# Rotary partner rows copied by SBUF transfers in place of permutation products

## The chip, the cores and the metric

The kernel runs on one core of a Trainium2 chip. The metric is the device time of one execution in microseconds (us). Engines are named as in the profile: PE (matrix products), PEld (its weight loads), DVE, ACT, POOL, and SP, which only issues transfers. ACT can issue transfers as well; such an issue is written ACTq.

## The reference

Two layers of a transformer block (512 tokens, width 1024) are followed by a second block with a recurrent mixer and a mixture of experts. The change touches only the attention of the two layers: of every head of 64 columns the first 16 are rotated by an angle that depends on the position.

```python
def partial_rotary(t, positions):
    inv_freq = ROPE_THETA ** (-jnp.arange(0, ROT_DIM, 2, dtype=jnp.float32) / ROT_DIM)
    ang = positions.astype(jnp.float32)[:, :, None] * inv_freq
    cos = jnp.cos(ang)[:, :, None, :]
    sin = jnp.sin(ang)[:, :, None, :]
    t1, t2, rest = tf[..., :half], tf[..., half:ROT_DIM], tf[..., ROT_DIM:]
    rot = jnp.concatenate([t1 * cos - t2 * sin, t2 * cos + t1 * sin, rest], axis=-1)
...
        proj = h @ w_in[l] + b_in[l]
        q, k, v, u = jnp.split(
            proj, [ATTN_WIDTH, ATTN_WIDTH + KV_WIDTH, ATTN_WIDTH + 2 * KV_WIDTH], axis=-1)
        q = partial_rotary(q.reshape(B, S, N_HEADS, HEAD_DIM), positions)
        k = partial_rotary(k.reshape(B, S, N_KV_HEADS, HEAD_DIM), positions)
...
        attn_out = sliding_window_attention_with_sinks(q, k, v, sinks[l])
        pool_out = causal_pool_mixer(u, pool_w[l], pool_scale[l])
        mix = jnp.concatenate([attn_out, pool_out], axis=-1) @ w_out[l]
```

The sliding window has 128 keys, there are 8 query heads and 2 key heads. The pool mixer works on the columns u of the same projection.

## The kernel before

Activations lie transposed in SBUF: features on the 128 partitions, the 512 tokens along the free axis. A block of 128 features holds two heads, and the rotated rows are 0 to 15 and 64 to 79. Every product of 32-bit numbers is made as three products of a high and a low part (`mm3`, L156 to L158); the high part is a copy by ACT (L121 for activations, L148 for weights), the low part a difference by DVE or POOL (L122, L149). Weights come in slabs of 1 MB that SP loads into three `raw` buffers; `w` is the split slab.

Each of the two layers begins with the projection (`part`, tiles `pj` and `pu`, 24 products of 128x512 for each block of 128 output columns). Five of its blocks are rotated: the keys k and the queries q0 to q3. So `rotary` (L534 to L548) runs ten times in all. One rotary before the change: ACT brings the block with its bias into `pr` (L537) and makes the high part `th` (L121); DVE makes the low part `tl` (L122); PE multiplies both with the permutation matrix `rot` into `rp` (L541, L542), which brings to each rotated row its partner row, 8 rows further up or down, with its sign; DVE multiplies `rp` with the sine table `sn1` into `ru` (L544); POOL multiplies `pr` in its own place with the cosine table `cs1` (L545); DVE adds both (L546). Then ACT and DVE split `ru` into the pair that the scores are made of (`Qh`, `Ql` for k, q0 and q1; `Gh`, `Gl` for q2 and q3).

The rotary is a generator that yields after `tl` has been issued, and `layer` writes other projection work between its two halves. The final order on each engine is that of a list scheduler that works with its own estimates of times; each engine then executes its list strictly in order. Buffers come from rings with a fixed number of places: `TA` (2 places) holds `pr`, `TB` (1) holds `ru`, `TH` and `TL` (4 each) hold the pairs `th`/`tl`. TH and TL are used by attention too: the transposed probabilities `pt` (L596) are split into `th` (L645) and `tl` (L656), and so are the pool mixer's tiles and the squares for the norms.

After q0 and q1 the first call of `attend` begins: for each of eight units the scores `sc` (L156 to L158 on `Qh`), a softmax (`s`, `nm`, `es`, `sm`; exponentials by ACT at L631), the transposes `pt`, then the product `pv` with v. Projection blocks of u and the pool mixer are put between them as filling work. In layer 0 the products of `mod` (L275, modulation of the later norms) run in the background, straight from 1 MB loads of `ada_w` (L266) in the same three `raw` buffers. `tables` (L877) makes `sn1` and `cs1` once; `load_consts` makes `rot` by five DVE instructions from the identity.

Of the kernel before, what the change touches and what calls it, by code (L numbers as in the profile page):

```python
# [10 lines left out]
F32 = mybir.dt.float32  # L11
F32R = mybir.dt.float32r
# [4 lines left out]
OP = mybir.AluOpType  # L17
# [53 lines left out]
class K:  # L71
# [95 lines left out]
    def load_consts(self):  # L167
        nc, A = self.nc, self.A
        if "c" in A:
            self.crow = self.const.tile([KB, 128], F32, name="crow")  # L170
            nc.sync.dma_start(self.crow, A["c"].rearrange("o (k p) -> (o k) p", p=128))
        t = self.const.tile([128, CONST_W], F32, name="cst")
        nc.sync.dma_start(t, A["cst"])
        self.c = {n: t[:, o:o + w] for n, (o, w) in CONST_COLS.items()}
        self.ident = self.c["ident"]
        self.ones = self.const.tile([128, 2], F32, name="ones")
        nc.vector.memset(self.ones, 1.0)
        self.rot = self.const.tile([128, 128], F32R, name="rotr")
        nc.vector.tensor_scalar(self.rot, self.ident, 0.0, None, op0=OP.mult)
        for h in (0, 64):  # L180
            nc.vector.tensor_scalar(self.rot[:, h:h + 8], self.ident[:, h + 8:h + 16], -1.0, None, op0=OP.mult)
            nc.vector.tensor_copy(self.rot[:, h + 8:h + 16], self.ident[:, h:h + 8])
        self.eps = self.const.tile([128, 1], F32, name="eps")
        nc.vector.memset(self.eps, EPS)
        self.halfpi = self.const.tile([128, 1], F32, name="halfpi")
        nc.vector.memset(self.halfpi, math.pi / 2)
# [347 lines left out]
    def rotary(self, p, bias, done):  # L534
        nc = self.nc
        t = self.blk("TA", F32, "pr")
        nc.scalar.activation(t, p, AF.Identity, bias=bias)  # L537
        th, tl = self.tsplit(t)
        yield
        p = self.ps("rp", tag="t")  # L540
        nc.tensor.matmul(p, lhsT=self.rot, rhs=th, start=True, stop=False)  # L541
        nc.tensor.matmul(p, lhsT=self.rot, rhs=tl, start=False, stop=True)  # L542
        u = self.blk("TB", F32, "ru")
        nc.vector.tensor_tensor(u, p, self.sn1, op=OP.mult)  # L544
        nc.gpsimd.tensor_tensor(t, t, self.cs1, op=OP.mult)  # L545
        nc.vector.tensor_tensor(u, u, t, op=OP.add)  # L546
        done(u)
        yield  # L548
# [326 lines left out]
                    self.norms(h, newF, gg, gs, sh, H)  # L875
        return H or newF

    B1 = dict(G=16, Q=12, U=4, TH=4, TL=4, TA=2, TB=1)
    W1 = dict(raw=3, w=4)

    def tables(self):
        nc, A = self.nc, self.A
        self.sn1, self.cs1 = self.sincos(A["positions"], self.c["inv1"], "r1")
        self.nsink = []
        for l in range(2):
            t = self.ph.tile([128, 8], F32, name=f"sink{l}")
            s = A["sinks"][l]
            nc.sync.dma_start(t, bass.AP(tensor=s.tensor, offset=s.offset, ap=[[0, 128], [1, 8]]))
            nc.vector.tensor_scalar(t, t, -1.0, None, op0=OP.mult)
            self.nsink.append(t)  # L890
# [471 lines left out]
class K3(K2):  # L1362
# [700 lines left out]
    def run(self, out, ctx):  # L2063
        self.load_consts()
        with self.phase("w1", **self.W1), ExitStack() as self.ctx, self.phase("hh", side="right", H=16):
            with self.phase("b1", side="right", **self.B1):
                H = self.block1()
# [27 lines left out]
```

## Time and profile before

| | us |
|---|---|
| median of three runs | 2533.7 (2531.62 to 2534.28) |
| the profiled execution | 2530.84 |
| its span, from first to last instruction | 2529.0 |
| PE busy in the span | 2408.8 (95%) |
| DVE / ACT / POOL busy | 1372.4 / 907.3 / 366.6 |

The profile comes from one execution, 2.9 us under the median, and 1.84 us of its time lie around the span. The mean granted clock of PE is 0.979 of full speed. The five rotaries of layer 0 lie between 64 and 101 us of the span, those of layer 1 between 642 and 672 us. In the timelines a row is: start, duration, engine, line and operation, out<-in, count; behind it in brackets the idle time of the engine before it, and what ended that.

### The profile page before, as it was taken

To read this page: it belongs to the slowest core of one execution; us is meant where nothing else is said; L and a number is where in the kernel's file an instruction comes from. 1 tells how busy PE (TensorE), PEld (TensorE's weight loads), DVE (VectorE), ACT (ScalarE), POOL (GpSimd) and SP (SyncE) were. 2 spreads that over 40 slices of the span, in tenths; PEclk is the share of its full clock that TensorE was granted. 3 is DMA by queue.
4 is the path that set the end of the run, shared out by engine and by line. 5 is a ranking of instruction groups with operands and counts; after the bars stand their busy time and mean duration, and the time that the engine had idled before them with its cause. 6 is when DMAs were issued, how large, how long until landed. Compare 5 with 4: busy or idle time off the path is not lost. (4 is left out here: it accounts for less than half of the span.)

```text
span 2529.0 us, 30517 instructions
## 1 busy us (share of the span) xinstructions
PE 2408.8 (95%) x11804; PEld 1757.0 (69%) x11804; DVE 1372.4 (54%) x2203; ACT 907.3 (36%) x1577; POOL 366.6 (14%) x358
## 2 busy tenths in 40 slices
PE   7999999999899999998999999999999999989996
PEld 3668777778788888887787787887887643433332
DVE  4867566437977233336788786356544444222224
ACT  3654232223664222224555555233332211112111
POOL 1324000005433000002332331010000000000000
PEclk9998999999998999999999999999999999999998
DMA  7531576432212233222121122222223599989995
GB/s 259 186 111 59 200 278 215 155 100 68 64 58 63 88 100 100 84 82 76 59 76 51 42 92 78 97 78 75 90 77 133 199 374 414 423 367 424 423 423 248
DMA packets 221295, 416.60 MB, mean 165 GB/s; under 512 B 11746, under 2 KB 185294, under 8 KB 193500
## 3 DMA queue, kind: packets, MB, share of 16 engines
q1 hardware_dynamic: 214752, 406.07, 44.3%
q0 software_dynamic: 2736, 5.83, 0.6%
q10 hardware_dynamic: 3660, 2.72, 0.4%
q8 instruction: 94, 1.54, 0.2%
q14 instruction: 53, 0.43, 0.0%
HBM read 414.01 MB, written 4.72 MB: 166 GB/s over the span
## 5 line engine op out<-in xcount | busy, mean ns | idle before, releaser
L149 DVE TENSOR_TENSOR w<-raw,w 128x1024 fp32r<-128x1024 f32 (+2 forms) x216 | 263.4, 1221 | 231.1 <-ACT w L148 231.1
L148 ACT ACTIVATE w<-raw 128x1024 fp32r<-128x1024 f32 (+2 forms) x228 | 229.0, 1010 | 375.0 <-PE pu L158 149.1
L156 PE MATMUL pj<-Hh,w 128*128 128x512 f32 (+1 forms) x704 | 280.8, 403 | 5.9 <-ACT Hh L392 3.5
L157 PE MATMUL pj<-Hl,w 128*128 128x512 f32 (+1 forms) x704 | 277.9, 396 | 6.8 <-DVE Hl L395 6.8
L158 PE MATMUL pj<-Hh,w 128*128 128x512 f32 (+1 forms) x704 | 274.0, 390 | 0.0
L1833 PE MATMUL gu<-ew,x 128*64 128x512 f32 (+2 forms) x1024 | 247.1, 599 | 0.0
L158 PE MATMUL po<-Gh,w 128*128 128x512 f32 (+1 forms) x608 | 212.4, 349 | 0.0
L156 PE MATMUL po<-Gh,w 128*128 128x512 f32 (+1 forms) x608 | 211.7, 349 | 0.5 <-ACT Gh L621 0.5
L157 PE MATMUL po<-Gl,w 128*128 128x512 f32 (+1 forms) x608 | 211.2, 347 | 0.0
L156 PE MATMUL pu<-Hh,w 128*128 128x512 f32 (+1 forms) x448 | 171.7, 383 | 0.1
L157 PE MATMUL pu<-Hl,w 128*128 128x512 f32 (+1 forms) x448 | 170.9, 381 | 0.0
L158 PE MATMUL pu<-Hh,w 128*128 128x512 f32 (+1 forms) x448 | 170.8, 382 | 0.0
L1833 PEld LDWEIGHTS gu<-ew,x 128*64 128x64 f32 (+2 forms) x1024 | 75.0, 134 | 136.0 <-issue 121.3
L157 PEld LDWEIGHTS pj<-Hl,w 128*128 128x128 f32 x704 | 135.5, 193 | 42.3 <-DVE Hl L395 9.1
L158 PEld LDWEIGHTS pj<-Hh,w 128*128 128x128 f32 x704 | 134.5, 191 | 35.5 <-issue 7.7
L156 PEld LDWEIGHTS pj<-Hh,w 128*128 128x128 f32 x704 | 134.5, 193 | 34.2 <-ACT Hh L392 4.6
L157 PE MATMUL pg<-Hl,w 128*128 128x512 f32 (+1 forms) x384 | 148.0, 386 | 7.2 <-DVE Hl L395 6.9
L156 PE MATMUL pg<-Hh,w 128*128 128x512 f32 (+1 forms) x384 | 146.8, 382 | 0.0
L158 PE MATMUL pg<-Hh,w 128*128 128x512 f32 (+1 forms) x384 | 146.7, 382 | 0.0
L1889 DVE SCALAR_TENSOR_TENSOR yl<-yp,wsm,yh 128x512 fp32r<-128x512 f32 x30 | 22.5, 751 | 212.0 <-ACT yh L1888 210.5
L1088 POOL TENSOR_TENSOR QP<-QP,tot 128x512 f32<-128x512 f32 x64 | 102.9, 1611 | 219.1 <-ACT Y L1081 171.1
L158 PEld LDWEIGHTS po<-Gh,w 128*128 128x128 f32 x608 | 114.4, 188 | 19.5 <-issue 4.2
(519 smaller groups left out, 4737.5 us busy)
## 6 DMA issues: line engine op xcount, KB each, us to landing
ew<-in_w SPq DMA_DIRECT2D x192, 1024.0 KB
raw<-in_w_in SPq DMA_DIRECT2D x34, 1024.0 KB
raw<-in_ada_w SPq DMA_DIRECT2D x24, 1024.0 KB
raw<-in_w_gate SPq DMA_DIRECT2D x22, 1024.0 KB
raw<-in_w_up SPq DMA_DIRECT2D x22, 1024.0 KB
raw<-in_ada_w SPq DMA_DIRECT2D x40, 512.0 KB
raw<-in_w_in SPq DMA_DIRECT2D x40, 512.0 KB
raw<-in_w_down SPq DMA_DIRECT2D x16, 1024.0 KB
```

Of the source, the lines that this page charges most:

```text
L148: nc.scalar.activation(hv[:, k], rv[:, k], AF.Copy)
L149: (nc.gpsimd if b in self.low else nc.vector).tensor_tensor(lv[:, k], rv[:, k], hv[:, k].bitcast(F32), op=OP.subtract)
L156: nc.tensor.matmul(out, lhsT=wh, rhs=ah, start=first, stop=False)
L157: nc.tensor.matmul(out, lhsT=wh, rhs=al, start=False, stop=False)
L158: return nc.tensor.matmul(out, lhsT=wl, rhs=ah, start=False, stop=last)
L1088: nc.gpsimd.tensor_tensor(w, w, self.other(TOT, h, seg=1), op=OP.mult)
L1833: self.plast = self.nc.tensor.matmul(out[n * j:n * j + n, :], lhsT=X[k // 4][:, k % 4 * 128 + n * j:k % 4 * 128 + n * j + n], rhs=w, start ...
L1889: v.scalar_tensor_tensor(lo, p, ws, hi.bitcast(F32), op0=OP.mult, op1=OP.subtract)
```

## The change

The matrix `rot` and its five DVE instructions go. In `rotary` the split of `pr` and the two products go. Instead four transfers from SBUF to SBUF, issued on ACT's queue, copy 8 rows of 512 numbers (16 KB) each from `pr` to one of two new tiles `partner` (128x512), which POOL sets to zero once in `tables`. DVE multiplies `partner` with `sn1`; the sign of the upper eight rows is put into `sn1` by two small DVE instructions in `tables`. TH and TL get 3 places in place of 4.

```diff
-        self.rot = self.const.tile([128, 128], F32R, name="rotr")
-        nc.vector.tensor_scalar(self.rot, self.ident, 0.0, None, op0=OP.mult)
-        for h in (0, 64):
-            nc.vector.tensor_scalar(self.rot[:, h:h + 8], self.ident[:, h + 8:h + 16], -1.0, None, op0=OP.mult)
-            nc.vector.tensor_copy(self.rot[:, h + 8:h + 16], self.ident[:, h:h + 8])
...
         t = self.blk("TA", F32, "pr")
         nc.scalar.activation(t, p, AF.Identity, bias=bias)
-        th, tl = self.tsplit(t)
-        yield
-        p = self.ps("rp", tag="t")
-        nc.tensor.matmul(p, lhsT=self.rot, rhs=th, start=True, stop=False)
-        nc.tensor.matmul(p, lhsT=self.rot, rhs=tl, start=False, stop=True)
+        r = self.partner[self.nrot % 2]
+        self.nrot += 1
+        for h in (0, 64):
+            nc.scalar.dma_start(r[h:h + 8, :], t[h + 8:h + 16, :])
+            nc.scalar.dma_start(r[h + 8:h + 16, :], t[h:h + 8, :])
+        yield
         u = self.blk("TB", F32, "ru")
-        nc.vector.tensor_tensor(u, p, self.sn1, op=OP.mult)
+        nc.vector.tensor_tensor(u, r, self.sn1, op=OP.mult)
         nc.gpsimd.tensor_tensor(t, t, self.cs1, op=OP.mult)
         nc.vector.tensor_tensor(u, u, t, op=OP.add)
...
-    B1 = dict(G=16, Q=12, U=4, TH=4, TL=4, TA=2, TB=1)
+    B1 = dict(G=16, Q=12, U=4, TH=3, TL=3, TA=2, TB=1)
...
         self.sn1, self.cs1 = self.sincos(A["positions"], self.c["inv1"], "r1")
+        for h in (0, 64):
+            nc.vector.tensor_scalar(self.sn1[h:h + 8, :], self.sn1[h:h + 8, :], -1.0, None, op0=OP.mult)
+
+        self.partner, self.nrot = [self.ph.tile([128, 512], F32, name=f"partner{i}") for i in range(2)], 0
+        for t in self.partner:
+            nc.gpsimd.memset(t, 0.0)
```

The lines of the changed kernel stand five lines higher from here on (`pr` at L532, the transfers at L536 and L537, POOL's product at L541, the score products still at L156 to L158). POOL writes `pr` in its place, so it waits until all four transfers have read it.

What the change moves shows on ACT in layer 1, from the query block q0 on. Before:

```order
L743 ACTIVATE Qh_5305<-vt_5392 128x4x64
L121 ACTIVATE th_5388<-pr_5386 128x512
L148 ACTIVATE w_5438<-raw_5433 128x1024
L121 ACTIVATE Qh_5297<-ru_5361 64x512
L121 ACTIVATE Qh_5301<-ru_5361 64x512
L743 ACTIVATE Qh_5309<-vt_5392 128x4x64
L537 ACTIVATE pr_5427<-pj_5164,vec_425 128x512
L121 ACTIVATE th_5429<-pr_5427 128x512
```

After, on the same engine in the same place:

```order
L739 ACTIVATE Qh_5290<-vt_5374 128x4x64
L536 DMA partner_444<-pr_5368 8x512
L537 DMA partner_444<-pr_5368 8x512
L121 ACTIVATE Qh_5282<-ru_5343 64x512
L121 ACTIVATE Qh_5286<-ru_5343 64x512
L536 DMA partner_444<-pr_5368 8x512
L537 DMA partner_444<-pr_5368 8x512
L739 ACTIVATE Qh_5294<-vt_5374 128x4x64
L532 ACTIVATE pr_5406<-pj_5149,vec_419 128x512
```

Two of q0's four issues stand ahead of the two `Qh` that end the keys' rotary, and two behind them. In the same way the last issue or issues of each later block stand behind the `Qh` or `Gh` of the block before.

On PE in layer 0, just after the first 96 projection products, before:

```order
L275 MATMUL mod_578<-raw_576,cact 32x512 x4
L275 MATMUL mod_578<-raw_583,cact 32x512 x4
L541 MATMUL rp_598<-th_572,rotr 128x512
L542 MATMUL rp_598<-tl_573,rotr 128x512
L738 MATMUL vt_617<-cst,pr_609 128x128 x4
L156 MATMUL pj_683<-Hh_218,w_592 128x512
L157 MATMUL pj_683<-Hl_219,w_592 128x512
```

And after:

```order
L270 MATMUL mod_578<-raw_576,cact 32x512 x4
L270 MATMUL mod_578<-raw_583,cact 32x512 x4
L156 MATMUL pj_677<-Hh_212,w_592 128x512
L157 MATMUL pj_677<-Hl_213,w_592 128x512
L270 MATMUL mod_578<-raw_637,cact 32x512 x4
L158 MATMUL pj_677<-Hh_212,w_592 128x512
L156 MATMUL pj_677<-Hh_214,w_592 128x512
```

The third group of `mod` products (on `raw_637`, a load of 1 MB) now stands behind two projection products, where before the keys' two `rp` products, `vt` and 14 projection products lay ahead of it.

On DVE in layer 1, around the first softmax units, before:

```order
L544 TENSOR_TENSOR ru_5555<-rp_5552,r1s 128x512
L546 TENSOR_TENSOR ru_5555<-ru_5555,pr_5533 128x512
L635 SCALAR_TENSOR_TENSOR s_5577<-sc_5567,cst 128x2x128
L639 TENSOR_REDUCE nm_5579<-s_5577 128x2
L122 TENSOR_TENSOR Gl_5560<-ru_5555,Gh_5559 128x512
```

And after, where the last rotary's product and sum stand:

```order
L644 RECIPROCAL sm_5564<-sm_5564 128x2
L540 TENSOR_TENSOR ru_5525<-partner_445,r1s 128x512
L643 TENSOR_TENSOR sm_5594<-sm_5594,es_5573 128x2
L552 TENSOR_TENSOR ws_5628<-pr_5626 128x511
L542 TENSOR_TENSOR ru_5525<-ru_5525,pr_5506 128x512
L644 RECIPROCAL sm_5594<-sm_5594 128x2
L652 TENSOR_TENSOR tl_5583<-pt_5579,th_5582 128x256
```

Before, the last rotary (q3) is done on DVE ahead of the first unit's mask and maximum (`s`, `nm`); now the first three units' masks and maxima stand ahead of it, and it stands ahead of the first unit's `tl`.

## Rows read from the trace of the kernel before

**Rows 1.** The page's part 1: busy us, share of the span, instructions.

```profile
PE 2408.8 (95%) x11804; PEld 1757.0 (69%) x11804; DVE 1372.4 (54%) x2203; ACT 907.3 (36%) x1577; POOL 366.6 (14%) x358
```

**Rows 2.** Windows: stretch, length, busy us (instructions) of each engine, granted clock, DMA share, GB/s.

```profile
core 0: us, PE busy (x) PEld busy (x) DVE busy (x) ACT busy (x) POOL busy (x), PEclk, DMA share, GB/s
0.00:20.00 20.00, 10.28 (x62) 6.44 (x62) 7.65 (x32) 10.03 (x24) 3.19 (x12) 1.00 0.91 310
...
60.00:80.00 20.00, 19.79 (x96) 11.67 (x94) 14.14 (x23) 11.65 (x19) 2.52 (x2) 1.00 0.66 233
...
180.00:600.00 420.00, 414.26 (x2028) 337.54 (x2028) 244.70 (x352) 133.65 (x196) 50.83 (x53) 0.98 0.48 162
640.00:660.00 20.00, 17.23 (x94) 13.84 (x93) 17.49 (x20) 14.12 (x22) 7.88 (x5) 1.00 0.24 67
```

**Rows 3.** Waits of PE: line waited for, us in total, times, longest.

```profile
PE rp L542 <- DVE tl L122: 8.2, 5, 2.3
...
PE ct L254 <- DMA cst<-in_cst: 3.9, 1, 3.9
```

**Rows 4.** Tile rp: count, ns min/median/max, first and last start, form.

```profile
L542 PE MATMUL rp<-tl,rotr x10: 392/498/697, 68.7 to 668.3; 128*128 128x512 f32 x10
```

**Rows 5.** Tile pr: the rotaries' work on ACT, DVE and POOL.

```profile
L121 ACT ACTIVATE th<-pr x10: 614/632/633, 65.3 to 664.8; 128x512 fp32r<-128x512 f32 x10
L122 DVE TENSOR_TENSOR tl<-pr,th x10: 677/682/2843, 65.9 to 667.6; 128x512 fp32r<-128x512 f32 x10
L545 POOL TENSOR_TENSOR pr<-pr,r1c x10: 1277/1610/2209, 74.2 to 668.4; 128x512 f32<-128x512 f32 x10
L546 DVE TENSOR_TENSOR ru<-ru,pr x10: 675/688/1879, 75.5 to 670.2; 128x512 f32<-128x512 f32 x10
```

**Rows 6.** Timeline of PE in layer 0, the stretch of the first two rotaries.

```profile
69.57 0.39 PE L157 MATMUL pj<-Hl,w 128*128 128x512 f32 x1
...
72.36 0.40 PE L157 MATMUL pj<-Hl,w 128*128 128x512 f32 x1
72.69 1.04 PE L275 MATMUL mod<-raw,cact 128*32 128x512 f32 x2
...
74.32 1.06 PE L275 MATMUL mod<-raw,cact 128*32 128x512 f32 x6
```

**Rows 7.** Timeline of PE in layer 1, around the last rotary.

```profile
668.33 0.70 PE L542 MATMUL rp<-tl,rotr 128*128 128x512 f32 x1 [2.33 <-DVE tl L122]
...
670.53 0.63 PE L157 MATMUL pu<-Hl,w 128*128 128x512 f32 x1
670.96 0.63 PE L158 MATMUL pu<-Hh,w 128*128 128x512 f32 x1
```

**Rows 8.** Timeline of ACT in layer 1: pr and Qh of k, then Qh of q0 and q1.

```profile
642.56 0.69 ACT L537 ACTIVATE pr<-pj,vec 128x512 f32<-128x512 f32 x1 [1.11 <-PE pj L158]
...
650.07 1.28 ACT L121 ACTIVATE Qh<-ru 64x512 fp32r<-64x512 f32 x2 [0.42 <-DVE ru L546]
...
657.79 0.63 ACT L121 ACTIVATE Qh<-ru 128x512 fp32r<-128x512 f32 x1 [1.71 <-DVE ru L546]
...
662.63 0.63 ACT L121 ACTIVATE Qh<-ru 128x512 fp32r<-128x512 f32 x1 [2.44 <-DVE ru L546]
```

**Rows 9.** Timeline of DVE: the first unit's low part, layer 0, then layer 1.

```profile
104.55 0.42 DVE L656 TENSOR_TENSOR tl<-pt,th 128x256 fp32r<-128x256 f32 x1
...
677.83 0.42 DVE L656 TENSOR_TENSOR tl<-pt,th 128x256 fp32r<-128x256 f32 x1
```

**Rows 10.** Transfers: timelines of ACT's and SP's issues, then tile xg's landings.

```profile
13.07 0.32 ACTq L195 DMA_DIRECT2D vecs<-in_ada_b  x1
...
16.54 0.28 ACTq L195 DMA_DIRECT2D vecs<-in_g_post_mix  x1
...
1.20 0.38 SPq L173 DMA_DIRECT2D cst<-in_cst  x1
...
67.59 1.20 SPq L266 DMA_DIRECT2D raw<-in_ada_w  x2
...
DMA to landing us min/median/max: 5.0/8.5/9.4
```

## The prediction

> **What bounds the kernel now.** I read part 1 of the page first: PE is busy for 95% of the span, every other engine for about half or less [rows 1]. Then the windows by stage. From 180 to 600 us, the feed-forward of layer 0, PE is busy for 414 of 420 us [rows 2]; nothing that the change does to ACT, DVE or the transfers can show there. In the stretch from 640 to 660 us, where the rotaries of layer 1 run, PE has 17.2 of 20 us and DVE 17.5 [rows 2]: there PE waits. The list of PE's waits names for whom: the second rotation product waits for DVE's `tl` in five of its ten executions, 8.2 us in all [rows 3]. The rotary tiles show ten such products, ten `th` and ten `tl` [rows 4, 5]. So the change takes away work from the engine that bounds, and the wait that stands in front of it. What takes the wait's place is the question.
>
> **What goes.** 20 PE products. Their durations overlap, so I price them by pitch: from 69.57 to 72.36 lie twelve steps of like products, 2.79 / 12 = 0.233 us each [rows 6]; 20 x 0.233 = 4.7 us. Waits for `tl`: 8.2 us. Ten `th` on ACT (10 x 0.63) and ten `tl` on DVE (10 x 0.68, one of them stretched to 2.84) are work beside PE [rows 5]. If nothing new ended later, the upper bound were 4.7 + 8.2 = 12.9 us. The products that follow the last of these waits (2.33 us at 668.33) run at a pitch of 670.96 - 670.53 = 0.43 instead of 0.23 us [rows 7], as at the lower of the clock's two levels (1.2 and 2.4 GHz); what this may cost or give is weighed with the third rival. The five constant instructions and the two new zeroings lie at the start, beside the first loads, where PE has 10.3 of 20 us [rows 2]: nothing.
>
> **What comes.** 40 issues on ACT. An issue of a small load there takes 0.32 us [rows 10]: 40 x 0.31 = 12.4 us of ACT against 6.3 us of `th` saved, on an engine busy for 36% [rows 1]. What counts is the latency. The trace has no transfer inside SBUF. The nearest rows: the load of `cst` is issued by 1.58 (1.20 + 0.38) [rows 10], and PE, idle for its first 3.9 us, starts when it has landed [rows 3]: 2.3 us, for far more than 16 KB. A 24 KB load issued by ACT by 13.39 lets the next one that uses its semaphore go only at 16.54 [rows 10]: 3.15 us, with the DMA engines at 0.91 [rows 2]. The far bound are the gathers of the expert stage, 5.0 us at best [rows 10]. From below: no transfer lands in less than nothing, and since a copied block needs no `tl`, a gain is possible. I take 2.0 us in layer 1 (DMA share 0.24) and 2.4 us in layer 0 (share 0.66) [rows 2], near the first row since both ends are on the chip and small; 3.15 for either is the bound that I keep for the range.
>
> By the Trainium skill (DMA: Bandwidth & Descriptors, Queues, rings and completion order) each DMA engine goes in turn through the queues for which it has work, packet by packet. By that a small copy on ACT's queue would pass SP's megabytes; layer 0 would then land like layer 1, and the sum would be 4 x 0.4 = 1.6 us lower. The 3.15 us beside a busy SP queue speak against taking it in full.
>
> **The new chain.** From `pr`: four issues (1.24), landing, POOL's product in place, which must wait for the transfers (1.61), DVE's sum (0.69) [rows 5]; then `Qh` (0.63). The order on ACT ties the blocks together: the second half of each block's issues stands behind the `Qh` of the block before, so one round from `Qh` to the next `Qh` is 0.63 + 0.62 + landing + 1.61 + 0.69 = 3.55 + landing, with no PE in it.
>
> Layer 1: `pr` of k ends at 643.25, a weight split (about 1.0) stands ahead of the issues, they end at 645.5, landing 647.5, POOL 649.1, sum and `Qh` at 649.8, against 650.07 before [rows 8]. `Qh` for k takes 1.28 (two halves): q0's second half is issued by 651.7, landed 653.7, `Qh` at 656.0, against 657.79. A round of 5.55 later q1's `Qh` is at 661.5, against 662.63 [rows 8]. For q2 three issues stand behind q1's `Qh` instead of two, so its `Gh` comes 5.86 later, near 667.4, and POOL's weight split (2.5 to 2.8) adds about 1.2 us there, by where it falls: 668.6. q3's issues end at 669.9, land at 671.9, POOL ends at 673.5, DVE's sum at 674.2. The first unit's `tl` stands behind this sum: 674.3 against 677.83 [rows 9]. This is -3.5 us. Before, that `tl` waited for scores that PE could begin only after all five `rp` pairs; now the scores start before q2 is rotated, so the softmax is no longer last. Landing enters about four times: it is +4 us for each microsecond.
>
> Layer 0: the keys must wait for the tables in any case. q0 to q3 go through the same rounds, with loads beside them; one of q3's transfers shares its semaphore with a 1 MB load of `ada_w` and waits until that is in. By the same steps the first `tl` falls at about 103.1 against 104.55 [rows 9], -1.4 us. PE gets one new wait: the third group of `mod` products stands early now, and its 1 MB is issued only from 67.59 on [rows 10]. In the old order that group began at 72.69 [rows 6] and did not wait. PE has 2.8 us less work ahead of it and will idle for 2 to 3 us there, but the work that it did in that time before is filling work, needed before the first `tl` anyway, so I count the wait as within the -1.4. The group was also cut in two by `rp`, at 1.04 and 1.06 us for two and six products [rows 6]; this goes.
>
> TH and TL with 3 places: attention and the pool mixer hold a pair each, so a `th` on ACT now waits for an older product on PE a few times. Bounds 0 and 2.5 us (about ten cases, a product's 0.23 us each); I take 1, on the side of PE's filling work that covers most.
>
> Sum: -3.5 - 1.4 + 1.0 = -3.9 us. From the profiled execution 2530.84 - 3.9 = 2526.9; the runs' median stands 2.9 above it, and 2533.7 - 3.9 = **2529.8 us**. Later stages pass this on, since PE bounds the next stage [rows 2]. With all landings at 3.15 us the sum is -3.9 + 4 x 0.75 + 4 x 1.15 = +3.7, with 1.5 us it is -9.5.
>
> **Rivals.** *The chain is covered and PE gets everything back.* The blocks' chains lie beside filling products that PE must make anyway; if the scheduler's order always has some ready, all of 4.7 + 8.2 less 1 us comes: -11.9, 2521.8. For it: PE is the bound over most of the span. Against it: the first `tl` hangs on five rounds with no PE in them, and filling work stands behind the scores in order.
>
> *The transfers land late (slower).* Four or five landings are in series in each layer. The sum crosses zero when they take 0.5 us longer than I took them for (3.9 / 8), 2.5 and 2.9 us; it passes +5 at 1.1 us longer, 3.1 and 3.5. At 4.0 everywhere: -3.9 + 4 x 1.6 + 4 x 2.0 = +10.5, 2544; at the gathers' 5.0, 2552. For it: 3.15 us in the one row beside a busy queue, and four transfers a block, each with a semaphore shared with loads. Against it: DMA share 0.24 in layer 1.
>
> *PE's clock takes the gain.* PE idles in places where it did not: for the load in layer 0 (2 to 3 us) and between scores and first transposes in layer 1 (about 4 us). After the 2.33 us wait of before it went at half pace for some 3.6 us [rows 7], a loss of 1.8. Two or three such stretches more cost 3.6 to 5.4: near 2534, no change. For it: that row. Against it: PE waited five times before, and only this one wait shows it.
>
> **How the numbers follow.** A measurement of this kernel can tell about 0.2%, 5.1 us, from no change. The forecast's case (the chain decides, -9.5 to +3.7) has 0.57: of it 0.22 below -5.1, the rest within. Full return 0.16, faster. Late landings 0.17, slower. Clock 0.10, within. That makes faster 0.38, same 0.45, slower 0.17. The range from 2521 to 2541 holds the forecast's case, the upper part of full return and the first half of late landings (to 3.7 us), and leaves out about 0.16.
>
> **What would show it.** Right: no `rp`; PE's waits for `tl` of `pr` gone; POOL's product waits for a transfer; from the last issue to POOL about 2.0 to 2.4 us; first `tl` of layer 1 near 674 and of layer 0 near 103; PE waits near 69 to 72 us for a load of `ada_w`. Wrong: landings over 3.1 us (slower), PE with no waits at all between 640 and 680 (full return), a granted clock under 0.9 in new stretches, or new waits at `th` of attention of more than 2.5 us in sum.

## The result, and the profile after

The changed kernel takes 2550.63 us (median of four runs, 2549.66 to 2551.75), the kernel before 2532.66 in the same comparison: a ratio of 1.0073, with a 95% interval of 1.006 to 1.0085. It is 18 us slower; the forecast was 2529.8, a gain of 3.9 us, and the range ended at 2541.

PE's busy time in the span is 2413.8 us (2408.8 before [rows 1]), though 20 products are gone. The mean granted clock fell from 0.979 to 0.971, and a product counts longer at the lower level (0.63 us for 128x512 at 670.53 [rows 7], 0.39 at 69.57 [rows 6]). The span is 2549.9 us, 20.9 more than before; 5.0 of that is busy time of PE and 15.9 idle. The windows show where (columns as in [rows 2]):

```profile
core 0: us, PE busy (x) PEld busy (x) DVE busy (x) ACT busy (x) POOL busy (x), PEclk, DMA share, GB/s
60.00:80.00 20.00, 15.00 (x68) 9.11 (x67) 12.49 (x21) 8.80 (x12) 1.78 (x1) 0.82 0.56 190
...
180.00:600.00 420.00, 413.95 (x1981) 333.64 (x1981) 244.94 (x345) 135.04 (x195) 45.62 (x46) 0.98 0.49 164
...
680.00:700.00 20.00, 11.11 (x40) 8.97 (x41) 15.59 (x30) 9.45 (x26) 7.05 (x9) 0.60 0.43 111
```

The feed-forward is as before, 414 of 420 us. From 60 to 80 us PE has 15.0 us busy (19.8 before [rows 2]) at a granted clock of 0.82, and from 680 to 700, where before the attention was under way, 11.1 us at 0.60. The tile of the partner rows shows what came in:

```profile
L536 ACTq DMA_DIRECT2D partner<-pr x20: 631/632/754, 66.3 to 690.8; - x20
L537 ACTq DMA_DIRECT2D partner<-pr x20: 631/632/637, 67.1 to 691.5; - x20
L540 DVE TENSOR_TENSOR ru<-partner,r1s x10: 691/693/2564, 74.1 to 693.6; 128x512 f32<-128x512 f32 x10
```

An issue of such a copy holds ACT's queue for 0.63 us, twice the 0.32 of the small load [rows 10]; forecast were 0.31.

One measure serves all kernels below: the time from the keys' `pr` to the first unit's `tl`, that is, from the first rotary to the first softmax brought through. It is read from one execution of each kernel. Before it is 104.55 - 64.53 = 40.0 us in layer 0 and 677.83 - 642.56 = 35.3 in layer 1 [rows 8, 9]. After, `pr` starts at 65.53 and 655.52, and DVE's timeline has

```profile
113.04 0.40 DVE L652 TENSOR_TENSOR tl<-pt,th 128x256 fp32r<-128x256 f32 x1
...
696.69 0.40 DVE L652 TENSOR_TENSOR tl<-pt,th 128x256 fp32r<-128x256 f32 x1
```

so 47.5 and 41.2 us: 7.5 and 5.9 us more. Of the 20.9 us between the two spans 13.4 lie in these two stretches, 1.0 before the first rotary and 3.6 right behind the first stretch: layer 0's output projection begins 47.7 us after that `tl` (113.04 to 160.7), and before it began 44.1 us after it.

How a round runs after the change is seen in layer 1, from q0 to q1 and on to q2. ACT's timeline:

```profile
664.82 0.63 ACT L121 ACTIVATE Qh<-ru 64x512 fp32r<-64x512 f32 x1 [1.10 <-DVE ru L542]
...
665.55 0.63 ACTq L537 DMA_DIRECT2D partner<-pr  x1
...
672.43 0.63 ACT L121 ACTIVATE Qh<-ru 128x512 fp32r<-128x512 f32 x1 [4.16 <-DVE ru L542]
672.43 0.64 ACTq L536 DMA_DIRECT2D partner<-pr  x1
673.12 0.63 ACTq L537 DMA_DIRECT2D partner<-pr  x1
...
681.55 0.63 ACT L121 ACTIVATE Qh<-ru 128x512 fp32r<-128x512 f32 x1 [4.66 <-DVE ru L542]
...
682.90 0.63 ACTq L537 DMA_DIRECT2D partner<-pr  x1
690.79 0.63 ACT L121 ACTIVATE Gh<-ru 128x512 fp32r<-128x512 f32 x1 [4.66 <-DVE ru L542]
```

DVE's, with the product on the partner tile and the sum of each block (the first and second row belong to q0 and q1):

```profile
667.65 0.69 DVE L540 TENSOR_TENSOR ru<-partner,r1s 128x512 f32<-128x512 f32 x1 [0.30 <-DMA partner<-pr]
...
676.86 0.69 DVE L540 TENSOR_TENSOR ru<-partner,r1s 128x512 f32<-128x512 f32 x1 [0.75 <-DMA partner<-pr]
...
678.71 2.81 DVE L542 TENSOR_TENSOR ru<-ru,pr 128x512 f32<-128x512 f32 x1 [1.16 <-POOL pr L541]
...
688.22 0.69 DVE L540 TENSOR_TENSOR ru<-partner,r1s 128x512 f32<-128x512 f32 x1 [1.04 <-DMA partner<-pr]
```

And POOL's, q1's product and the weight split behind it:

```profile
676.90 1.78 POOL L541 TENSOR_TENSOR pr<-pr,r1c 128x512 f32<-128x512 f32 x1 [5.05 <-DMA partner<-pr]
678.64 2.34 POOL L149 TENSOR_TENSOR w<-raw,w 128x1024 fp32r<-128x1024 f32 x1
```

q0's last issue ends at 666.18 and DVE reads the partner rows at 667.65: the copies land in 1.5 us. q1's last two issues start with q0's `Qh` at 672.43, though q1's `pr` had been there since 667.33, and end at 673.75. They land at 676.86, 3.1 us later; POOL's product takes 1.78; DVE's sum takes 2.81 instead of 0.69, since POOL's weight split started 0.07 us before it; then comes q1's `Qh`, at 681.55. The round has 9.1 us, where the forecast had 5.55. q2's round has 9.2 (690.79 - 681.55), with a landing of 4.7 (from 683.53 to 688.22).

The stretched sums are waits for POOL. q1's sum ends at 681.52, 0.54 us after POOL's split (680.98). The keys' product on the partner tile shows the same with another length:

```profile
660.49 1.98 POOL L541 TENSOR_TENSOR pr<-pr,r1c 128x512 f32<-128x512 f32 x1 [7.30 <-DMA partner<-pr]
```

```profile
661.24 1.78 DVE L540 TENSOR_TENSOR ru<-partner,r1s 128x512 f32<-128x512 f32 x1
```

It started 0.75 us after POOL and ended 0.55 after it (663.02 and 662.47). Where DVE starts first, as at 676.86 against POOL's 676.90, it takes 0.69 us. So the length depends on how long POOL's operation still has to run, and on the order in which the two start.

Layer 0 has long landings too. DVE's timeline for the keys and for q3:

```profile
74.10 0.69 DVE L540 TENSOR_TENSOR ru<-partner,r1s 128x512 f32<-128x512 f32 x1 [2.20 <-DMA partner<-pr]
...
110.49 0.69 DVE L540 TENSOR_TENSOR ru<-partner,r1s 128x512 f32<-128x512 f32 x1 [2.09 <-DMA partner<-pr]
```

ACT's last issues had ended at 69.06 and 107.08: 5.0 and 3.4 us. (The keys' landing can have cost only part of its 5.0, since POOL had the cosine table only at 74.04.) From `Qh` to `Qh` the rounds of layer 0 have 9.7, 8.9 and 8.5 us (the last ends with q2's `Gh`), and q1's `Qh` comes 2.2 us after its sum, behind two weight splits on ACT.

PE meanwhile stands still in layer 1:

```profile
682.24 0.47 PE L156 MATMUL sc<-Qh,Qh 128*128 128x128 f32 x1 [4.95 <-ACT Qh L121]
...
693.68 0.69 PE L592 MATMUL pt<-cst,s 128*128 128x128 f32 x2 [5.81 <-ACT s L650]
```

It waits 4.95 us for q1's `Qh` and 5.81 us for the first softmax, and the products after each wait run at the lower of the two clock levels (the granted clock from 680 to 700 is 0.60).

### The profile page after: what moved, and what is told of

Read it like the earlier page. It is cut to its first block, busy times and chain, and to the rows that moved or that the text cites. A ratio compares the mean times of both kernels' runs of the same rounds, so it can differ in the third digit from the quotient of the medians.

```text
span 2549.9 us, 30539 instructions
## 1 busy us (share of the span) xinstructions
PE 2413.8 (95%) x11784; PEld 1760.9 (69%) x11784; DVE 1369.9 (54%) x2190; ACT 902.8 (35%) x1567; POOL 365.8 (14%) x360
## 3 DMA queue, kind: packets, MB, share of 16 engines
q8 instruction: 93, 1.52, 0.2%
## 5 line engine op out<-in xcount | busy, mean ns | idle before, releaser
L156 PE MATMUL pj<-Hh,w 128*128 128x512 f32 (+1 forms) x704 | 281.2, 404 | 8.5 <-ACT Hh L387 3.4
L158 PE MATMUL pj<-Hh,w 128*128 128x512 f32 (+1 forms) x704 | 274.6, 391 | 1.3 <-DVE w L149 1.3
L156 PE MATMUL po<-Gh,w 128*128 128x512 f32 (+1 forms) x608 | 212.1, 349 | 0.5 <-ACT Gh L617 0.5
L158 PE MATMUL po<-Gh,w 128*128 128x512 f32 (+1 forms) x608 | 211.7, 348 | 0.0
L156 PE MATMUL pu<-Hh,w 128*128 128x512 f32 (+1 forms) x448 | 172.8, 386 | 0.2
L158 PE MATMUL pu<-Hh,w 128*128 128x512 f32 (+1 forms) x448 | 172.0, 385 | 0.0
L158 PEld LDWEIGHTS pj<-Hh,w 128*128 128x128 f32 x704 | 134.7, 192 | 38.0 <-issue 6.8
L156 PEld LDWEIGHTS pj<-Hh,w 128*128 128x128 f32 x704 | 134.7, 193 | 37.7 <-ACT Hh L387 4.6
L156 PE MATMUL pg<-Hh,w 128*128 128x512 f32 (+1 forms) x384 | 146.7, 382 | 0.0
L158 PE MATMUL pg<-Hh,w 128*128 128x512 f32 (+1 forms) x384 | 146.6, 382 | 0.0
L156 PEld LDWEIGHTS po<-Gh,w 128*128 128x128 f32 x608 | 114.3, 188 | 22.0 <-issue 5.0
```

Source lines behind the costliest of these rows:

```text
L156: nc.tensor.matmul(out, lhsT=wh, rhs=ah, start=first, stop=False)
L158: return nc.tensor.matmul(out, lhsT=wl, rhs=ah, start=False, stop=last)
```

## The experiments

All times are medians, with the ratio to the kernel before in the same comparison. In these comparisons the kernel before has medians between 2529.54 and 2532.67 us, so the ratios compare better across rows than the times do. The last two columns are the measure from `pr` to `tl`; e13 leaves layer 0 as it was and shows 46.6 there against 47.5, so about a microsecond between two rows says nothing.

| kernel | us | ratio (95%) | layer 0 | layer 1 |
|---|---|---|---|---|
| before | 2532.66 | | 40.0 | 35.3 |
| after | 2550.63 | 1.0073 (1.006 to 1.0085) | 47.5 | 41.2 |
| e1, no copies | 2530.67 | 0.9998 (0.9988 to 1.0008) | 39.5 | 34.0 |
| e2, issues only | 2530.19 | 0.9994 (0.9984 to 1.0003) | 40.7 | 33.6 |
| e3, POOL beside | 2544.63 | 1.005 (1.0033 to 1.0066) | 45.0 | 38.2 |
| e4, before, rings of 3 | 2531.24 | 0.9996 (0.9986 to 1.0006) | 41.5 | 35.2 |
| e5, narrow copies | 2541.48 | 1.0035 (1.0021 to 1.005) | 46.2 | 38.0 |
| e6, two queues | 2534.92 | 1.001 (1.0 to 1.002) | 41.0 | 35.5 |
| e7, layer 1 only | 2540.54 | 1.0034 (1.0023 to 1.0046) | 40.0 | 41.1 |
| e8, before, fp32 product | 2533.38 | 1.0005 (0.9995 to 1.0015) | 38.9 | 32.5 |
| e9, all on SP | 2538.45 | 1.0024 (1.0014 to 1.0034) | 40.2 | 35.2 |
| e10, two queues, POOL beside | 2531.45 | 0.9997 (0.9987 to 1.0007) | 37.2 | 34.0 |
| e11, before, POOL beside | 2538.08 | 1.0021 (1.0011 to 1.0031) | 43.9 | 33.6 |
| e12, loads held | 2555.11 | 1.0099 (1.0082 to 1.0116) | 55.0 | 42.5 |
| e13, w_out late | 2548.97 | 1.0065 (1.0052 to 1.0079) | 46.6 | 38.8 |

**e1: what is there to win.** The four transfers are left out.

```diff
-        for h in (0, 64):
-            nc.scalar.dma_start(r[h:h + 8, :], t[h + 8:h + 16, :])
-            nc.scalar.dma_start(r[h + 8:h + 16, :], t[h:h + 8, :])
```

> The changed kernel without its 40 transfers: the partner tiles stay zero, so the rotation's sine term is left out. Landing theory (the transfers' latency, in series from block to block, is the loss) and issue theory (the 0.63 us that each of the 40 issues takes on ACT, with weight splits behind them, is the loss): both expect 5 to 13 us less than before, 2520 to 2528. Ring theory (TH and TL with 3 places cost): 2540 or more, since the rings are as in the changed kernel.

All three theories missed: it is neither faster nor slower than before. No product, no `th`, no `tl`, no transfer, and the first `tl` of layer 1 comes 34.0 us after `pr` instead of 35.3. PE's waits have only moved. Its timeline and DVE's in layer 1:

```profile
667.87 0.39 PE L156 MATMUL sc<-Qh,Qh 128*128 128x256 f32 x1 [2.32 <-ACT pr L532]
...
675.72 0.69 PE L589 MATMUL pt<-cst,s 128*128 128x128 f32 x2 [1.52 <-ACT s L647]
```

```profile
652.23 3.42 DVE L149 TENSOR_TENSOR w<-raw,w 128x1024 fp32r<-128x1024 f32 x1
...
663.90 2.68 DVE L539 TENSOR_TENSOR ru<-ru,pr 128x512 f32<-128x512 f32 x1
...
677.17 0.42 DVE L649 TENSOR_TENSOR tl<-pt,th 128x256 fp32r<-128x256 f32 x1
```

PE now waits 2.32 us until ACT has read a block (`pr`), and 1.52 us for the first softmax. DVE has 16.4 of 20 us from 660 to 680, among it a sum of 2.68 us, and at 652.23 it has a weight split of 3.42, both stretched beside POOL. So the wait for `tl` that the list names [rows 3] was the place where PE met a backlog, not the cause of it. e8 says the same in another way:

```diff
-        self.rot = self.const.tile([128, 128], F32R, name="rotr")
+        self.rot = self.const.tile([128, 128], F32, name="rotr")
...
-        th, tl = self.tsplit(t)
         yield
         p = self.ps("rp", tag="t")
-        nc.tensor.matmul(p, lhsT=self.rot, rhs=th, start=True, stop=False)
-        nc.tensor.matmul(p, lhsT=self.rot, rhs=tl, start=False, stop=True)
+        nc.tensor.matmul(p, lhsT=self.rot, rhs=t, start=True, stop=True)
```

> The kernel before with the rotation as one product of 32-bit numbers with the permutation, not split: ten th, ten tl and the waits for tl go, PE works a little longer for each block, no transfer is added. If PE's wait for tl and the work of the splits were worth their 8 us, as the prediction's terms had it: 2522 to 2528. If the stretch is held by the chain of DVE and ACT to the first softmax, as the run without copies says: 2529 to 2534, no change.

The measure falls to 38.9 and 32.5 us, and the kernel's time does not follow (2533.4, as the second expectation had it). In its trace the time is lost again between the two stretches: the keys' `pr` of layer 1 starts at 644.72, before at 642.56. The ratio's interval holds 1.

**e2: issues without landings.** The copies go to a tile that nothing reads; POOL writes to `ru` and DVE multiplies in place, as in e3 (these three lines are left out here).

```diff
-        r = self.partner[self.nrot % 2]
+        r, d = self.partner
         self.nrot += 1
         for h in (0, 64):
-            nc.scalar.dma_start(r[h:h + 8, :], t[h + 8:h + 16, :])
-            nc.scalar.dma_start(r[h + 8:h + 16, :], t[h:h + 8, :])
+            nc.scalar.dma_start(d[h:h + 8, :], t[h + 8:h + 16, :])
+            nc.scalar.dma_start(d[h + 8:h + 16, :], t[h:h + 8, :])
```

> The 40 issues stay, but copy into a tile that nothing reads, so nobody waits for a landing to read it (the sine term is left out; POOL's product goes to ru and no longer waits for the transfers). Landing theory: near the kernel without copies, 2522 to 2532. Issue theory: near the changed kernel, 2543 to 2551.

40 issues of 0.63 us cost nothing by themselves, as the landing theory expected. The closest comparison is with e3, whose edit differs only in the tile that the copies go to, which DVE reads there: 2544.63 - 2530.19 = 14.4 us for waiting on the landings, measured side by side. The windows add a second thing:

```profile
60.00:80.00 20.00, 16.16 (x74) 9.80 (x75) 12.94 (x22) 9.91 (x14) 2.38 (x2) 0.83 0.56 185
80.00:100.00 20.00, 20.00 (x109) 14.27 (x109) 14.01 (x19) 9.69 (x14) 10.00 (x7) 1.00 0.73 258
```

PE loses the same time from 60 to 80 us as in the changed kernel (16.2 us busy, clock 0.83), since the order there is the same, and makes it good at once: 20.0 of 20 us after it. So the new standstill of layer 0, which the timeline of the changed kernel shows as

```profile
67.45 1.92 PE L270 MATMUL mod<-raw,cact 128*32 128x512 f32 x16
72.02 0.50 PE L156 MATMUL pj<-Hh,w 128*128 128x512 f32 x1 [2.64 <-ACT w L148]
...
73.80 1.94 PE L270 MATMUL mod<-raw,cact 128*32 128x512 f32 x8 [1.04 <-DMA raw<-in_ada_w]
...
77.05 0.79 PE L158 MATMUL pj<-Hh,w 128*128 128x512 f32 x1 [1.31 <-DVE w L149]
```

(2.64 us for a weight split that ACT makes only after the four issues, 1.04 for the load of `ada_w`, 1.31 for DVE) is not where the time goes: the kernel becomes slow when it also waits for the landings.

**e3: POOL beside the transfers.**

```diff
-        nc.vector.tensor_tensor(u, r, self.sn1, op=OP.mult)
-        nc.gpsimd.tensor_tensor(t, t, self.cs1, op=OP.mult)
-        nc.vector.tensor_tensor(u, u, t, op=OP.add)
+        nc.gpsimd.tensor_tensor(u, t, self.cs1, op=OP.mult)
+        nc.vector.tensor_tensor(r, r, self.sn1, op=OP.mult)
+        nc.vector.tensor_tensor(u, u, r, op=OP.add)
```

> The changed kernel with POOL's product written to ru instead of in place, so that POOL works while the transfers are under way and DVE multiplies the partner tile in its place: POOL's 1.7 us leave each of the five rounds of a layer. Landing theory: 8 to 16 us less than the changed kernel, 2535 to 2543. Issue theory: the order of issues is what costs, so at most 4 us less, 2546 to 2551.

6.0 us come back (2550.63 - 2544.63), between the two expectations: POOL's place in the round counts, and is about a third of the loss.

**e4: the rings.** TH and TL at 3 places in the kernel before.

```diff
-    B1 = dict(G=16, Q=12, U=4, TH=4, TL=4, TA=2, TB=1)
+    B1 = dict(G=16, Q=12, U=4, TH=3, TL=3, TA=2, TB=1)
```

> The kernel before with TH and TL at 3 places and nothing else. Ring theory: at least half of the 18 us, 2541 or more. Landing and issue theory: within 3 us of the kernel before, 2530 to 2536; the prediction's term was +1 (0 to 2.5).

No change: the ring theory falls.

**e6 and e9: who issues.** In e6 the copies for rows 64 on go to SP's queue; in e9 all four do.

```diff
-        for h in (0, 64):
-            nc.scalar.dma_start(r[h:h + 8, :], t[h + 8:h + 16, :])
-            nc.scalar.dma_start(r[h + 8:h + 16, :], t[h:h + 8, :])
+        for h, e in ((0, nc.scalar), (64, nc.sync)):
+            e.dma_start(r[h:h + 8, :], t[h + 8:h + 16, :])
+            e.dma_start(r[h + 8:h + 16, :], t[h:h + 8, :])
```

> The changed kernel with two of each block's four issues on SP's queue, the other two on ACT's. If what makes the chain long is also that ACT issues one after the other and holds the second pair behind the Qh of the block before: 1.3 us and more leave each round, 2536 to 2544. If only landing counts: 2546 to 2552; and slower than the changed kernel (over 2553) if SP's weight loads now wait behind its two issues.

> The changed kernel with all four issues of a block on SP's queue: still one after the other, but ACT issues none, and the weight loads of SP stand behind a block's copies in order instead of beside them. If what costs is the tie on ACT (a block's last issues behind the Qh of the block before) and the weight stream beside the copies: as with two queues or up to 4 us more, 2533 to 2540. If it is the four issues of 0.63 us in a row, which stay: 2543 to 2551.

With two queues 15.7 of the 18 us are gone, more than either expectation, with SP alone 12.2, although there the four issues still follow one another. DVE stood idle for the partner rows for 8.3 us in all in the changed kernel, for 2.5 in e6 and 0.2 in e9: here the copies have mostly landed before their turn comes. In e9 the last copy of q0 is issued long before the keys' `Qh`, here on SP's and on ACT's timeline:

```profile
651.88 0.79 SPq L537 DMA_DIRECT2D partner<-pr  x1
```

```profile
655.06 1.29 ACT L121 ACTIVATE Qh<-ru 64x512 fp32r<-64x512 f32 x2 [2.38 <-DVE ru L542]
...
660.54 0.63 ACT L121 ACTIVATE Qh<-ru 128x512 fp32r<-128x512 f32 x1 [2.53 <-DVE ru L542]
...
666.37 0.63 ACT L121 ACTIVATE Qh<-ru 128x512 fp32r<-128x512 f32 x1 [3.67 <-DVE ru L542]
...
671.19 0.63 ACT L121 ACTIVATE Gh<-ru 128x512 fp32r<-128x512 f32 x1 [1.01 <-DVE ru L542]
```

From `Qh` to `Qh` (k, q0, q1, q2) it is 5.5, 5.8 and 4.8 us, 16.1 in sum; in the changed kernel, whose keys' `Qh` starts at 664.82, it is 7.6, 9.1 and 9.2, 26.0 in sum. The copies of a block now lie beside the block before it. Stretched sums are still there, and do not keep these kernels from coming near the time before. DVE's in e9, for the keys and for q1:

```profile
652.47 2.56 DVE L542 TENSOR_TENSOR ru<-ru,pr 128x512 f32<-128x512 f32 x1
...
663.69 2.64 DVE L542 TENSOR_TENSOR ru<-ru,pr 128x512 f32<-128x512 f32 x1
```

e6 has two as well, of 2.71 and 2.81 us. In e9 SP's weight loads stand behind the copies. Its traced execution is the fastest of ten (2533.28 us against the median of 2538.45), so its rows cannot show where the 5.8 us over before come from; that the held loads are the price is not shown.

**e12 and e13: the weight loads beside the copies.** With SP as issuer the loads of `w_out` are also held back. To tell this from ACT's order, e12 adds a fifth copy of one row on SP, which makes SP wait for each block.

```diff
+        nc.sync.dma_start(r[127:128, :], t[127:128, :])
```

> The changed kernel, its four issues a block on ACT as they are, with a fifth small copy of one row (2 KB, of a row whose sine is zero) on SP's queue. It does nothing but make SP wait for each block before it goes on with the weight loads: the weight stream is paced as with two queues, while ACT's order of layer 1 stays that of the changed kernel. With two queues 16 of the 18 us came back. If the weight stream beside the copies is at least half of that: 2543 or less. If it is the order on ACT (last issues behind the Qh of the block before, four issues in a row): 2546 to 2551.

It is slower than the changed kernel (by 4.5 us in the medians, by more in the ratios: 1.0099 against 1.0073), outside both expectations, and does not tell: in layer 1 the first load of `w_out` now starts at 673.89, just ahead of q1's last two copies, and they land in 3.6 us (675.76 to 679.40). Most of what it lost lies in layer 0 (55.0 against 47.5). So e13 lets the first slab of `w_out` in layer 1 wait for the last `Gh`:

```diff
+                if l and j == 0:
+                    for hh in range(2):
+                        nc.gpsimd.tensor_copy(t[64 * hh:64 * hh + 1, 0, 0:1], q[3][0][64 * hh:64 * hh + 1, 0:1].bitcast(F32))
+                    nc.gpsimd.tensor_copy(t[0:1, 4, 0:1], q[3][0][0:1, 0:1].bitcast(F32))
                 for hh in range(2):
```

> The changed kernel with the first loads of w_out in layer 1 made to wait for the last block's Gh (POOL first writes three elements of their buffer, taken from Gh), so that no weight load runs beside the copies of layer 1; ACT's order in layer 1 is that of the changed kernel, word for word, and layer 0 is as it was. If the weight stream beside the copies lengthens their landing: landings of q1 and q2 fall from 3.1 and 4.7 to about 1.5 us, and 4 to 6 us come back, 2544 to 2547. If it is the order on ACT alone: 2549 to 2552. If the weights then come too late for the output projection: over 2553.

The same four microseconds in the changed kernel and in e13, with the DMA share and GB/s at the end:

```profile
672.00:676.00 4.00, 3.30 (x15) 2.32 (x15) 2.20 (x3) 2.84 (x4) 0.00 (x0) 1.00 0.59 145
```

```profile
672.00:676.00 4.00, 3.67 (x18) 2.98 (x18) 2.88 (x3) 3.10 (x4) 1.82 (x1) 1.00 0.05 10
```

The stream is gone, and q1's copies land in 1.5 us again, from ACT's last issue (ending at 672.67) to POOL:

```profile
672.04 0.63 ACTq L537 DMA_DIRECT2D partner<-pr  x1
```

```profile
674.18 2.00 POOL L541 TENSOR_TENSOR pr<-pr,r1c 128x512 f32<-128x512 f32 x1 [3.40 <-DMA partner<-pr]
```

q1's landing did what the first expectation said, the time what the second said: 1.7 us come back (2550.63 - 2548.97) instead of 4 to 6, and the intervals of the two ratios overlap, so even these are not clear of noise. The measure in layer 1 falls from 41.2 to 38.8; the rounds are 7.6, 8.1 and 7.9 us. (One of the nine loads was not held: it starts at 678.95, beside q2's copies.) The loads beside the copies lengthen the landing, as the rows show, but by the measure they are the smaller part of the loss in layer 1, some 2.4 of 5.9 us. By the same measure POOL's place gives 3.0 (e3), and of the kernels that wait for their copies only those with copies on SP's queue get all of it back (e6, e9, e10). That ACT's order makes up the larger part is argued from the rounds; no run changed that order alone.

**e5, e7, e10, e11.** In e5 each copy has 64 columns instead of 512:

```diff
-            nc.scalar.dma_start(r[h:h + 8, :], t[h + 8:h + 16, :])
-            nc.scalar.dma_start(r[h + 8:h + 16, :], t[h:h + 8, :])
+            nc.scalar.dma_start(r[h:h + 8, :64], t[h + 8:h + 16, :64])
+            nc.scalar.dma_start(r[h + 8:h + 16, :64], t[h:h + 8, :64])
```

> The changed kernel with each transfer cut to the first 64 of its 512 columns (2 KB instead of 16 KB; the other columns' sine term is left out). If a transfer's price is its latency, whatever its size: 2546 to 2552, as the changed kernel. If it is its bytes, queued behind the weight loads: at least half of the 18 us come back, 2541 or less.

Half of the loss comes back, which lies between the two expectations, and it does not separate bytes from order: with its shorter copies the scheduler also put three of q0's four issues ahead of the keys' `Qh` in layer 1, not two.

e7 keeps the products in layer 0 (`if self.lay in COPY`, with `COPY = (1,)`).

> Copies in layer 1 only, products with the permutation in layer 0 (the sign moved to the sine table in both). The traces of the changed kernel and of before stand 12 to 13 us apart when layer 1 begins and 20 at its end. So the landing theory expects 6 to 9 us over before, 2537 to 2541; a loss that sits in one of the layers alone would show as 2532 or 2550.

The loss of layer 1 alone is 8.4 us (2540.54 - 2532.19), as expected; so both layers carry about half, as the traces said.

e10 joins e6's two queues with e3's order of the three products; e11 makes e3's edit in the kernel before, with DVE's product in place in PSUM.

> Copies on two queues and POOL's product written to ru, beside the transfers. POOL beside gave back 6 of 18 us where the copies ran on ACT alone; if the rounds of copies still decide with two queues, the same 3 to 6 us come here and it is even with before or better, 2528 to 2533. If the first softmax is now held by DVE and the splits, as without copies: 2530 to 2535.

> The kernel before with POOL's product written to ru and DVE's product in place in PSUM, so that POOL need not wait until th and tl are made. If the rotary's chain to the first scores holds this stretch: 3 to 8 us less than before, 2524 to 2530. If DVE and the weight splits hold it: no change, 2530 to 2534.

e10 is even with the kernel before, the best that copies reached here; both of its expectations allow that time, so it does not decide between them. e11 is 5.4 us slower, against both expectations; its measure is 3.9 us longer in layer 0 and 1.7 shorter in layer 1, and why stays open. No version beat the kernel before.

## Why the prediction was wrong

*What goes.* The count was right (20 products, ten `th`, ten `tl`), the worth was not. The prediction took 12.9 us as the upper bound and full return as a rival at 2521.8; with no copies at all the kernel stands at 2530.67, even with before. It read the wait for `tl` as a cost that goes with `tl`. DVE's busy share of that stretch, 17.5 of 20 us, stood in the same row as PE's [rows 2], and said that DVE was as near to being the bound as PE.

*What comes.* Landing was sized at 2.0 us in layer 1 and 2.4 in layer 0. With little else under way it is 1.5 to 1.6 us; beside a stream of weight loads it is 3.1 and 4.7 in layer 1 and 5.0 and 3.4 in layer 0. The DMA engines' share was 0.89 to 1.00 in those four landings, and at most 0.52 in the short ones. The issue was sized by a load's 0.31 us and is 0.63; e2 shows that this by itself costs nothing. The Trainium skill (DMA: Bandwidth & Descriptors, Queues, rings and completion order) has each DMA engine go in turn through the queues for which it has work. From this the prediction worked out a case in which a small copy passes the loads and layer 0 lands like layer 1; the rows (3.1 to 5.0 us beside streams of loads against 1.5) do not show that.

*The round.* This is the step that failed. The prediction saw the tie on ACT and put a round at 3.55 us and the landing. Measured were 7.6, 9.1 and 9.2 us in layer 1. For q0 to q1 the terms are: two issues 1.3 (forecast 0.63 and 0.62, together the same), landing 3.1 (2.0), POOL 1.8 (1.6), the sum 2.8 (0.7). The largest mis-sized term of that round is DVE's sum, at 0.69 in the prediction: its row [rows 5] had a longest of 1.88, and `tl` in the same rows one of 2.84. The prediction put 1.2 us for POOL's weight split into one round and left DVE's sum at its median in all five. From the keys' `Qh` to the first `tl` of layer 1 it had 24.5 us (649.8 to 674.3); the trace has 31.9 (664.82 to 696.69). Of the 7.4 us more, two stretched sums are 4.3, less the 1.2 allowed; the four landings together 2.8 (1.5, 3.1, 4.7 and 1.5 against 2.0 each), POOL's four products 0.7. Before the keys' `Qh` 2.1 us more were lost (9.3 from `pr` against 7.2). The prediction also had the softmax no longer last; PE's longest wait there, 5.81 us, is for it. A stretched sum alone is not the loss, though: e6 and e9 have two each in layer 1, and with copies on SP's queue their measure there is 35.5 and 35.2 us, that of before (35.3). By its price of about 8 us for each microsecond of landing, copies that land at once would have made the kernel some 20 us faster than before; the run without copies stands at the time before.

*Layer 0.* The wait for the load of `ada_w` came (1.04 us, forecast 2 to 3), and one for ACT's weight split that was not foreseen (2.64). Counting it as covered was right, as e2 shows. The first `tl` came at 113.04, not 103.1: this layer lost the most, 7.5 us up to that `tl`, and the prediction had not worked its rounds out one by one. Its rounds of 9.7, 8.9 and 8.5 us hold long landings, stretched operations on DVE and waits on ACT behind weight splits; no run tells these apart there.

*TH and TL.* +1 us (0 to 2.5) was forecast; e4 has no change. Nothing else depended on it.

*The rivals.* Late landing had the right sign and 0.17 of the chance. Its price per microsecond (about 8 for both layers, four landings in each, though the steps for layer 1 have five in series) would need landings of 4.9 us throughout for 18 us over before; the rows show 1.5 to 5.0, and five of the nine that can be read are 1.5 or 1.6. So that this rival had the right sign is in part luck: its price holds the landing responsible for what the rest of the round did as well. The clock's part is seen too (0.82 and 0.60 in the windows), as a follower of PE's waits; what it adds of its own was not measured.

*What is settled and what is not.* The loss needs the wait for the landings (e1 and e2 against the rest; e2 against e3 14.4 us), and most of it needs all copies on ACT's queue (e6 and e9): 12 to 16 of the 18 us. Moving copies to SP also spaces out SP's weight loads, so these two runs do not separate ACT's order from the loads. Taking most of the weight stream away in layer 1 gives 1.7, not clear of noise, POOL out of the round 6.0; these overlap, and the parts are not additive. The tie itself, with the copies still on ACT, was not untied in a run, and how much of layer 0's loss is its weight loads is open.

## What to carry to other kernels

A wait that the profile names can go to the next engine in line, as it did here with DVE at 17.5 of 20 us; look at all engines' busy time in the same window before counting the wait as a gain. Where a small transfer takes the place of a product, price the whole round through the issuing engine's order: what stands ahead of the issue in its list, and what that waits for. Price each DVE step by what POOL starts just ahead of it, not by its median. If the issuing engine also makes the result of the round before, try the issue on a queue that has nothing to do with it; here that was worth 12 to 16 us.

## What the runs showed of the hardware that was not expected

A copy of 8x512 numbers inside SBUF takes 0.63 us to issue, on ACT and on SP alike (medians), and lands 1.5 to 1.6 us after the issue ends when little else runs; beside streams of weight loads it took 3.1 to 5.0 us. DVE operations of 0.69 us that start just after POOL's weight split take 2.6 to 2.9 us and end 0.54 to 0.55 us after it (2.81 at 678.71, POOL from 678.64 to 680.98). It is a wait for POOL's operation to end and not a constant factor, and a median does not show it.
